# Four Strassen pairs per down projection, norms on ScalarE, beta by accumulating transfers, wider up-stage operations, and a planner that replays its order

## The chip, the cores and the metric

The kernel runs on one core of one Trainium2 chip. The metric is the device time of one execution in microseconds (us), given as the median of several runs. A core has five engines that work side by side: PE (matrix products, with PEld for its weight loads), DVE (VectorE), ACT (ScalarE), POOL (GpSimd) and SP (SyncE, which here only issues transfers). Each works through its own queue in order and waits on semaphores for the others.

## The reference

Two decoder layers over 256 tokens of width 1024, all in float32. `alpha` is a constant; every sub-layer ends in a layer norm with a gain (gamma) and a bias (beta).

```python
for i in range(2):
    y = chunked_gmlp(x, ...) if i == 0 else moba_attention(x, ...)
    x = layer_norm(DN_ALPHA * x + y, ln_mix_g[i], ln_mix_b[i])
    y = conv_ffn(x, f_w_up[i], f_conv_w[i], f_conv_b[i], f_w_down[i])
    x = layer_norm(DN_ALPHA * x + y, ln_ffn_g[i], ln_ffn_b[i])

def conv_ffn(x, w_up, conv_w, conv_b, w_down):   # w_up 1024 x 5632, w_down 2816 x 1024
    h = x @ w_up
    hc = conv_b + sum of three causally shifted h, each times its conv_w[j]
    g, val = jnp.split(hc, 2, axis=-1)
    return (jax.nn.gelu(g) * val) @ w_down
```

## The kernel before, in words

**Products of float32.** Every float32 operand of a large product is split into a high part and a low remainder of a faster type (`split`: ACT copies to the high part, DVE subtracts to get the low one). A product is then three matmuls: high x high, high x low, low x high. The weights arrive in chunks of 1 MB (`prep`), each 128 x 2048, are split into `whi` and `wlo`, and are held five chunks ahead. The activations are split too and live in `xt` (inputs of the up stages) or `rr` (inputs of the down stages).

**Stages.** PE runs a_v, a_u, a_out (mixer A), f_up0, f_dn0 (ConvFFN of layer 0), b_v, b_qk, b_o (mixer B), f_up1, f_dn1. A down projection (`project_out`) sums over 22 tiles `k` of 128 rows for two token halves `t` and two column halves. Two neighbouring `k` are a pair, so there are 11 pairs, and an ordinary pair takes 2 x 2 x 2 x 3 = 24 matmuls of 512 columns.

**Strassen pairs.** Pairs listed in `FAST` take seven products in place of eight (`unit`, 21 matmuls). For these, DVE builds four sums of weight blocks (`weight_forms`, four forms of 512 columns) and four sums of token blocks (`token_forms`), and both are split like any operand. The forms of the weights take the place of `xt` or of the used-up start of `rr` (`used_up`). Products that belong to no single output are kept in four PSUM banks (`sums`) and are added to the residual rows `x` by `combine` after the last fast pair.

**Up stages.** `conv_up` makes four output tiles of 256 columns per group (`cols_times`, ten groups a stage). Each lands in a PSUM bank as two halves that `join` adds (ACT copies one half, DVE adds the other). `gate` then applies the convolution (one ACT operation and two DVE operations per tile), the gelu, the product and the split.

**Inner norms.** After a_out, f_dn0 and b_o, `stats` computes mean and variance on DVE, POOL takes the power -0.5 (line L571), and `ln_back` normalizes the rows on DVE (`ts`, line L325), lets PE transpose them (L306), and lets ACT apply gamma and beta from `lncol` in the transposed layout and split the result to `xt`. `rest` later multiplies the rows by gamma and adds beta on DVE, since the rows are the next residual.

**What sets the order.** Nothing is issued when it is written. `Plan` records every operation with its engine, a cost in ns and what it depends on. `emit` gives PE's bulk matmuls in their written order a due time, walks the dependencies back to give all others theirs, then simulates the five queues once and emits the operations in the order of their simulated starts. PE work marked `fill` (transposes, attention scores) is fitted in when ready. Line L300 is where all matmuls are issued, L306 all transposes, L312 all ACT operations, L318 and L322 DVE's two-input ones, L329 SP's loads.

Of the kernel before, what the change touches and what calls it, by code (L numbers as in the profile page):

```python
# [53 lines left out]
FAST = {"f_dn0": (4, 7), "f_dn1": (4, 5, 7)}  # L54
# [24 lines left out]
class Op:  # L79
    __slots__ = ("i", "eng", "ns", "emit", "deps", "bufs", "fill", "due", "start", "end", "table", "nbytes", "rank")  # L80


class Plan:
# [4 lines left out]
    LATE = {"pe": 200.0, "act": 140.0, "dve": 130.0, "pool": 200.0, "sp": 910.0}  # L88
# [39 lines left out]
    def emit(self):  # L128
        ops = self.ops
        for o in ops:  # L130
            for b in o.bufs:
                for q in b.prev:
                    o.deps.update(x for x in q.ops if x is not o)
            assert all(d.i < o.i for d in o.deps), "a group waits for one recorded after it"

        t = 0.0
        for o in ops:
            o.due = math.inf
            if o.eng == "pe":
# [11 lines left out]
        succ, left = {}, {}
        for o in ops:
            left[o] = len(o.deps)
            for d in o.deps:
                succ.setdefault(d, []).append(o)
        engines = ("pe", "act", "dve", "pool", "sp")
        free = dict.fromkeys(engines, 0.0)
        cand = {e: [] for e in engines}
        bus, table = 0.0, None
        order = []  # L160
        bulk = [o for o in ops if o.eng == "pe" and not o.fill]
        nb = 0

        def ready(o):
            return max([0.0] + [d.end + self.lag(d, o) for d in o.deps])

        for o in ops:
            if not left[o]:
                cand[o.eng].append((0.0, o))
        while len(order) < len(ops):  # L170
            best = None
            for e in engines:
                c = cand[e]
                if e == "pe":
                    c = [x for x in c if x[1].fill or (nb < len(bulk) and x[1] is bulk[nb])]
                if not c:
                    continue
                s0 = min(max(free[e], r) for r, _ in c)
                now = [x for x in c if max(free[e], x[0]) <= s0 + 1.0]
                if e == "pe":  # L180
                    pick = min(now, key=lambda x: (not x[1].fill, x[1].due))
                else:
                    pick = min(now, key=lambda x: x[1].due + (x[1].ns if e in ("act", "dve") else 0.0))
                    for x in c:
                        s = max(free[e], x[0])
                        if x[1].due < pick[1].due and s0 < s < s0 + pick[1].ns and \
                                s + x[1].ns <= pick[1].due and x[1].due < s0 + pick[1].ns:
                            pick = x
                s = max(free[e], pick[0])
                if best is None or s < best[0]:  # L190
                    best = (s, e, pick)
            s, e, pick = best
            o = pick[1]
            cand[e].remove(pick)
            if o.eng == "pe" and not o.fill:
                nb += 1
            o.start = s
            if e == "sp":
                bus = max(bus, s + 1100.0) + o.nbytes / 415.0
                free[e] = max(s + 475.0, bus - 1500.0)  # L200
                o.end = bus
            else:
                extra = 0.0
                if o.table and o.table != table:
                    extra, table = 1300.0, o.table
                o.end = free[e] = s + o.ns + extra
            order.append(o)
            for x in succ.get(o, ()):
                left[x] -= 1
                if not left[x]:  # L210
                    cand[x.eng].append((ready(x), x))
        order.sort(key=lambda o: (o.start, o.i))
        for o in order:
            o.emit()
# [15 lines left out]
def trunk_kernel(ctx: ExitStack, tc: tile.TileContext, a: dict, out: bass.AP):  # L230
# [43 lines left out]
    banks = [ps.tile([P, HALF], F32, name=f"bank{i}") for i in range(BANKS)]  # L274
# [3 lines left out]
    def bank(long=False):  # L278
# [378 lines left out]
    def project_out(name, nk, at, xold, li, rows_i, wait=REST, first=None):  # L657
# [55 lines left out]
        def combine():  # L713
# [14 lines left out]
            for b in sums:  # L728
                done_with(b, 0)
# [414 lines left out]
```

## Time and profile before

| what | value |
|---|---|
| runs, us | 559.74, 557.76, 557.22 (median 557.76) |
| profiled execution: span from first to last instruction | 555.0 us |
| lowest and median run over that span | 2.2 us and 2.8 us |
| PE busy | 547.0 us, 99% |
| DVE busy | 498.9 us, 90% |
| ACT busy | 378.3 us, 68% |
| DMA, mean | 200 GB/s |

The time of the profiled execution itself is known only as its span; what lies around it is taken as the difference to the median, 2.8 us. Busy time counts an instruction from its start to its written result, and neighbours on one engine overlap a little, so a mean duration is longer than the step from one start to the next.

### The profile page before, as it was taken

To read this page: it belongs to the slowest core of one execution; us is meant where nothing else is said; L and a number is where in the kernel's file an instruction comes from. 1 tells how busy PE (TensorE), PEld (TensorE's weight loads), DVE (VectorE), ACT (ScalarE), POOL (GpSimd) and SP (SyncE) were. 2 spreads that over 40 slices of the span, in tenths; PEclk is the share of its full clock that TensorE was granted. 3 is DMA by queue.
4 is the path that set the end of the run, shared out by engine and by line. 5 is a ranking of instruction groups with operands and counts; after the bars stand their busy time and mean duration, and the time that the engine had idled before them with its cause. 6 is when DMAs were issued, how large, how long until landed. Compare 5 with 4: busy or idle time off the path is not lost.

```text
span 555.0 us, 8220 instructions
## 1 busy us (share of the span) xinstructions
PE 547.0 (99%) x2968; PEld 468.8 (84%) x2968; DVE 498.9 (90%) x967; ACT 378.3 (68%) x718; POOL 11.3 (2%) x17
## 2 busy tenths in 40 slices
PE   9999999999999999999999999999999999999994
PEld 6888888898988988888888888888898988988884
DVE  6889889999999999989948898889898999999997
ACT  6846586877877884645668877587767877776510
POOL 0010000000000000001000000000000000000001
PEclk9999999999999999999999999999999999999998
DMA  8996626686545524764565363416765466444602
GB/s 317 413 335 238 230 92 228 227 308 224 208 172 188 191 77 153 285 227 152 191 263 191 110 251 138 174 70 233 298 232 223 155 227 227 153 151 153 220 9 76
DMA packets 20105, 111.12 MB, mean 200 GB/s; under 512 B 2256, under 2 KB 5600, under 8 KB 7904
## 3 DMA queue, kind: packets, MB, share of 16 engines
q1 hardware_dynamic: 19488, 109.94, 54.7%
q10 hardware_dynamic: 576, 0.66, 0.3%
q8 instruction: 23, 0.38, 0.3%
q14 instruction: 18, 0.15, 0.1%
HBM read 109.52 MB, written 1.07 MB: 199 GB/s over the span
## 4 chain that ended last, share of the span: by engine, by line
PE 99%; DVE 1%; issue 0%; DVEq 0%
PE bank L300 96%; PE bank L306 2%; DVE x L322 0%; DVE stat L563 0%; DVEq L1140 0%; DVE stat L569 0%
## 5 line engine op out<-in xcount | busy, mean ns | idle before, releaser
L318 DVE TENSOR_TENSOR wlo<-raw,whi 128x1024 fp32r<-128x1024 f32 (+2 forms) x205 | 216.6, 1079 | 19.9 <-ACT whi L312 13.3
L312 ACT ACTIVATE whi<-raw 128x1024 fp32r<-128x1024 f32 (+2 forms) x205 | 185.1, 941 | 61.5 <-DMA raw<-in_f_up 22.2
L300 PE MATMUL bank<-xt,whi 128*128 128x512 f32 x832 | 195.9, 391 | 0.0
L300 PEld LDWEIGHTS bank<-xt,whi 128*128 128x128 f32 x832 | 154.2, 188 | 30.6
L300 PE MATMUL bank<-whi,rr 128*128 128x512 f32 (+1 forms) x428 | 134.1, 387 | 0.0
L300 PEld LDWEIGHTS bank<-xt,wlo 128*128 128x128 f32 x832 | 103.1, 192 | 2.1
L300 PE MATMUL bank<-xt,wlo 128*128 128x256 f32 x832 | 104.8, 284 | 0.0
L300 PEld LDWEIGHTS bank<-whi,rr 128*128 128x128 f32 x428 | 80.0, 188 | 16.2 <-issue 0.2
L300 PE MATMUL bank<-wlo,rr 128*128 128x512 f32 (+1 forms) x214 | 82.6, 386 | 0.0
L322 DVE SCALAR_TENSOR_TENSOR ff<-ff,convc 128x255 f32<-128x255 f32 (+1 forms) x160 | 70.4, 476 | 0.3 <-ACT ff L312 0.2
L312 ACT ACTIVATE ff<-bank 128x256 f32<-128x256 f32 (+2 forms) x126 | 49.3, 400 | 27.1 <-PE bank L300 19.9
L300 PE MATMUL bank<-whi,xt 128*128 128x512 f32 (+1 forms) x196 | 60.7, 390 | 0.0
L318 DVE TENSOR_TENSOR ff<-bank,ff 128x256 f32<-128x256 f32 (+1 forms) x110 | 45.5, 431 | 8.5 <-ACT ff L312 7.7
L312 ACT ACTIVATE ff<-ff,convc 128x256 f32<-128x256 f32 x80 | 45.0, 592 | 3.0 <-DVE ff L318 2.9
L300 PEld LDWEIGHTS bank<-wlo,rr 128*128 128x128 f32 x214 | 40.2, 188 | 7.9
L300 PEld LDWEIGHTS bank<-whi,xt 128*128 128x128 f32 x196 | 36.4, 188 | 8.3 <-ACT whi L312 1.2
L300 PE MATMUL bank<-wlo,xt 128*128 128x512 f32 (+1 forms) x98 | 36.4, 387 | 0.0
L312 ACT ACTIVATE ff<-bank,lncol 128x128 f32<-128x128 f32 x48 | 18.7, 459 | 17.5 <-PE bank L306 17.5
L318 DVE TENSOR_TENSOR ff<-ff 128x256 f32<-128x256 f32 (+3 forms) x74 | 30.3, 431 | 0.3 <-ACT ff L312 0.2
L312 ACT ACTIVATE ff<-ff 128x256 f32<-128x256 f32 x52 | 20.4, 411 | 11.3 <-DVE rr L318 6.8
L318 DVE TENSOR_TENSOR xt<-ff,xt 128x256 fp32r<-128x256 f32 (+3 forms) x32 | 21.8, 691 | 4.1 <-ACT xt L312 4.0
L312 ACT ACTIVATE rr<-ff 128x256 fp32r<-128x256 f32 (+3 forms) x50 | 21.3, 442 | 5.2 <-DVE ff L318 5.1
(75 smaller groups left out, 360.7 us busy)
## 6 DMA issues: line engine op xcount, KB each, us to landing
raw<-in_f_up SPq DMA_DIRECT2D x44, 1024.0 KB, 4.8
raw<-in_f_dn SPq DMA_DIRECT2D x20, 1024.0 KB, 4.8
raw<-in_b_qk SPq DMA_DIRECT2D x8, 1024.0 KB, 4.9
lnrow<-in_lnrow SPq DMA_DIRECT2D x5, 1024.0 KB, 6.6
raw<-in_a_u SPq DMA_DIRECT2D x4, 1024.0 KB, 8.4
raw<-in_a_out SPq DMA_DIRECT2D x4, 1024.0 KB, 6.0
raw<-in_b_v SPq DMA_DIRECT2D x4, 1024.0 KB, 4.7
raw<-in_b_o SPq DMA_DIRECT2D x4, 1024.0 KB, 4.9
```

What stands on the lines that cost most here:

```text
L300: nc.tensor.matmul(o, l, x, start=start, stop=stop, skip_group_check=mixed)
L306: nc.tensor.transpose(o, x, ident.ap)
L312: plan.op("act", ns, lambda: nc.scalar.activation(o, x, func, **kw), r, w, table=table)
L318: dve(70 + 1.04 * flat(x), lambda: nc.vector.tensor_tensor(o, x, y, op=op), r, w)
L322: lambda: nc.vector.scalar_tensor_tensor(o, x, s, y, op0=op0, op1=op1), r, w)
```

## The change

It does six things.

1. `FAST` names four pairs in each down projection, (3, 5, 6, 7), where it was two in f_dn0 and three in f_dn1. The raw weights of these pairs go to homes of their own (`home`): two places in `ff` and the tile `lnrow`, loaded in two transfers of 512 KB. `weight_forms` now works in place on the raw weights, in fewer and wider operations, and is recorded at points set by `FORMS`. `ln_rows` of a down projection is therefore loaded after `combine`.
2. The inner norms are made by ACT: DVE computes `shift` = -mean x rstd (one column), and ACT computes rstd x x + shift.
3. After a_out and b_o, beta is added to the rows by POOL, as a transfer from DRAM that accumulates into the rows; the multiplication by gamma stays on DVE.
4. In the up stages a group's four tiles lie in four neighbouring banks (`four_banks`); one ACT copy and one DVE addition of 1024 columns join them, and gelu, product and split work on 512 columns.
5. `build_bias` is recorded before f_up0 in place of after it.
6. `Plan.emit` orders 4 x 40 times, each time replays the order under four cases of speed, moves operations that PE waited for to earlier due times, and keeps the order with the smallest mean time. Matmuls, transposes and transfers have measured costs (`took`) beside the old ones.

```diff
-FAST = {"f_dn0": (4, 7), "f_dn1": (4, 5, 7)}
+FAST = {"f_dn0": (3, 5, 6, 7), "f_dn1": (3, 5, 6, 7)}
+HOMES = (0, 1, 2, 0, 1)
+FORMS = ((0, None), (1, 3), (0, 3), (1, 5))
 ...
+    def weight_forms(name, j):
+        key = name, FAST[name][j]
+        (r0, r1), f, (b11, b12, b21, b22) = raw_sums[key]
+        h, l = used_up(0, KT) if FORMS[j][0] else xt_new()
+        tt(f[:, b22:b12 - 1:b12 - b22, :], f[:, b12:b12 + 1, :].to_broadcast([P, 2, HALF]),
+           f[:, b22:b11 - 1 if b11 else None:b11 - b22, :], ALU.add, ...)
+        tt(f[:, b11, :], f[:, b22, :], f[:, b11, :], ALU.add, ...)
+        tt(f[:, b21, :], f[:, b11, :], f[:, b21, :], ALU.add, ...)
+        for n, raw in ((1, r1), (0, r0)):
+            split(...)
 ...
     def ln_back(r, st, mean, rstd, rows, t, li, h, l, waits, wait):
+        shift = st.ap[:, 28:29]
+        dve(70, lambda: nc.vector.scalar_tensor_tensor(shift, mean, -1.0, rstd, op0=ALU.mult, op1=ALU.mult), ...)
         for k0 in range(0, KT, step):
-            ts(x[:, sl], x[:, sl], mean, rstd, ALU.subtract, ALU.mult, ...)
+            act(x[:, sl], x[:, sl], AF.Identity, ..., bias=shift, scale=rstd)
         def rest():
             rb, rv = rows
+            if li != 1:
+                for o in (0, HALF):
+                    tt(x[:, sl], x[:, sl], rv[:, 0, sl], ALU.mult, ...)
+                beta = bass.AP(tensor=src.tensor, offset=..., ap=[[0, P], [1, D]])
+                plan.op("pool", 1000.0, lambda: nc.gpsimd.dma_start(x, beta, accum_op=ALU.add), ...)
+                return
 ...
+        if units:
+            weight_forms(name, 0)
+        def more(c):
+            for j, (_, after) in enumerate(FORMS[:len(units)]):
+                if c == after:
+                    weight_forms(name, j)
 ...
         for i in range(2, FT, 2):
-            tiles4 = [(bank(), *sub(name, i + j // 2, j % 2)) for j in range(4)]
-            cols_times(tiles4, h, l)
+            whole, four = four_banks()
+            cols_times([(b, *sub(name, i + j // 2, j % 2)) for j, b in enumerate(four)], h, l)
+            act(c3, b3[:, :, S:], AF.Copy, four, [c], psum=True)
+            tt(c3, b3[:, :, :S], c3, ALU.add, [*four, c], [c])
 ...
+        for seed in range(TRIALS):
+            for _ in range(ROUNDS):
+                order = self.order(self.dues(urge), seed)
+                runs = [self.replay(order, *case) for case in CASES]
+                mean = sum(r[0] for r in runs) / len(runs)
+                if best is None or mean < best[0]:
+                    best = mean, order
 ...
+                for _, waits in runs:
+                    for k, ns in waits:
+                        urge[k] += rnd.uniform(0.3, 1.0) * ns + rnd.uniform(0.0, 300.0)
```

Three places of the order follow. First PE in f_dn0 at pair 3. Before, the pair is ordinary, and these are the twelve matmuls of its first tile `k` (`whi_69`, `wlo_79`); twelve of the same kind on `whi_70` and `wlo_80` follow.

```order
L300 MATMUL bank_105<-whi_69,rr 128x512
L300 MATMUL bank_105<-wlo_79,rr 128x512
L300 MATMUL bank_105<-whi_69,rr 128x512
L300 MATMUL bank_106<-whi_69,rr 128x512
L300 MATMUL bank_106<-wlo_79,rr 128x512
L300 MATMUL bank_106<-whi_69,rr 128x512
L300 MATMUL bank_107<-whi_69,rr 128x512
L300 MATMUL bank_107<-wlo_79,rr 128x512
L300 MATMUL bank_107<-whi_69,rr 128x512
L300 MATMUL bank_108<-whi_69,rr 128x512
L300 MATMUL bank_108<-wlo_79,rr 128x512
L300 MATMUL bank_108<-whi_69,rr 128x512
```

The same pair after, whole: `small` holds the token forms, `xt_87` the weight forms.

```order
L358 MATMUL bank<-whi_70,rr 128x512
L358 MATMUL bank<-wlo_80,rr 128x512
L358 MATMUL bank<-whi_70,rr 128x512
L358 MATMUL bank<-whi_70,small 128x512
L358 MATMUL bank<-wlo_80,small 128x512
L358 MATMUL bank<-whi_70,small 128x512
L358 MATMUL bank<-whi_69,rr 128x512
L358 MATMUL bank<-wlo_79,rr 128x512
L358 MATMUL bank<-whi_69,rr 128x512
L358 MATMUL bank<-xt_87,rr 128x512 x3
L358 MATMUL bank<-xt_87,small 128x512 x9
```

Twenty-four matmuls have become 21, and the last twelve of them need the weight forms. Second the norm of the second token half after a_out. Before, on DVE (`stat_94` is that half's statistics, `x_89` its rows):

```order
L569 BN_AGGR stat_94<-stat_94 128x2
L318 TENSOR_TENSOR wlo_83<-raw_85,whi_73 128x512
L325 TENSOR_SCALAR x_89<-x_89,stat_94 128x256 x4
L318 TENSOR_TENSOR wlo_83<-raw_85,whi_73 128x512
L318 TENSOR_TENSOR wlo_84<-raw_85,whi_74 128x512
L318 TENSOR_TENSOR xt_87<-ff,xt_87 128x2x128 x2
```

After, on ACT (`ff<-bank,lncol` is gamma and beta on the transposed rows):

```order
L370 ACTIVATE x_89<-x_89,stat_94 128x256 x4
L370 ACTIVATE ff<-bank,lncol 128x128 x2
L370 ACTIVATE xt_87<-ff 128x2x128
L370 ACTIVATE ff<-bank,lncol 128x128 x2
L370 ACTIVATE xt_87<-ff 128x2x128
L1007 COPY ff<-bank 128x512
L370 ACTIVATE ff<-bank,lncol 128x128 x2
L370 ACTIVATE xt_87<-ff 128x2x128
```

The four pieces of the norm have moved from DVE to ACT, where they stand ahead of the operations on the transposed rows. Third POOL's queue from the first norm of a_out on. Before:

```order
L571 TENSOR_TENSOR stat_91<-stat_91,nhalf 128x1
L571 TENSOR_TENSOR stat_92<-stat_92,nhalf 128x1
L571 TENSOR_TENSOR stat_93<-stat_93,nhalf 128x1
L571 TENSOR_TENSOR stat_94<-stat_94,nhalf 128x1
L571 TENSOR_TENSOR stat_91<-stat_91,nhalf 128x1
```

After:

```order
L655 TENSOR_TENSOR stat_91<-stat_91,nhalf 128x1
L655 TENSOR_TENSOR stat_92<-stat_92,nhalf 128x1
L655 TENSOR_TENSOR stat_93<-stat_93,nhalf 128x1
L696 DMA x_88<-in_lnrow 128x1024
L655 TENSOR_TENSOR stat_94<-stat_94,nhalf 128x1
L696 DMA x_89<-in_lnrow 128x1024
```

The accumulating transfer of the first token half now stands ahead of the second half's power.

More of the change, by code (lines that the diff above doesn't have):

```diff
@@ L1 @@
 import math
+import random
 from contextlib import ExitStack
@@ L151, in emit @@
[L151 to L158, printed above, removed]
-        bus, table = 0.0, None
[L160 to L201, printed above, removed]
@@ new lines, in emit, with dues @@
+        for k in best[1]:
+            ops[k].emit()
+    def dues(self, urge):
+        ops, t = self.ops, 0.0
+        due = [math.inf] * len(ops)
+        for k, o in enumerate(ops):
+            if o.eng == "pe":
+                due[k] = t
+                t += o.took
+        for k in range(len(ops) - 1, -1, -1):
+            due[k] = min(due[k], t) - urge[k]
+            for d, late in self.deps[k]:
+                p = ops[d]
+                due[d] = min(due[d], due[k] - late - p.took - p.tail - (2000.0 if p.eng == "sp" else 0.0))
+        return [due[k] if o.rank is None else o.rank - 1e6 for k, o in enumerate(ops)]
@@ new lines, in replay @@
+    def replay(self, order, rate, first, act, dve):
+        ops, waits = self.ops, []
+        end = [0.0] * len(ops)
+        free = {"pe": BEGIN, "act": 0.0, "dve": 0.0, "pool": 0.0, "sp": 0.0}
+        by = {"act": act, "dve": dve}
+        bus, table = 0.0, None
+        for k in order:
+            o = ops[k]
+            e = o.eng
+            f = s = free[e]
+            for d, late in self.deps[k]:
+                s = max(s, end[d] + late)
+            if e == "pe" and s > f + 50.0 and s > 20000.0:
+                waits.append((k, s - f))
+            if o.nbytes:
+                bus = max(bus, s + first + (900.0 if e == "pool" else 0.0)) + \
+                    o.nbytes / 1000.0 / (rate if o.nbytes >= 1 << 20 or s < 80000.0 or e != "sp" else 0.72 * rate)
+                end[k], free[e] = bus, s + (380.0 if e == "sp" else o.took)
@@ L202, in emit @@
             else:
-                extra = 0.0
                 if o.table and o.table != table:
[L205 to L214, printed above, removed]
+                    s, table = s + 1300.0, o.table
@@ L284, in bank, with four_banks @@
         return b
+    def four_banks():
+        free = [i for i in (0, 4) if not any(x[2] for x in bank_of[i:i + 4])]
+        i = min(free, key=lambda i: max(x[0] for x in bank_of[i:i + 4]))
+        return psum[:, i * HALF:(i + 4) * HALF], [bank(at=j) for j in range(i, i + 4)]
     def done_with(b, age=None):
@@ L369, in trunk_kernel, with home @@
     xrows = [Buf(t) for t in xs_]
+    raw_sums = {}
+    def home(i):
+        name, c = stream[i]
+        j = HOMES[FAST[name].index(c)]
+        if j < 2:
+            pair, t, at = [place("ff", o + SUB * j, SUB) for o in (0, 5 * HALF)], ff, (0, 1, 5, 6)
+            at = [x + 2 * j for x in at]
+        else:
+            old, t, at = rowring.held[0], rowring.tiles[0], (0, 1, 2, 3)
+            group = rowring.held[0] = Buf(old.ap, [old])
+            pair = [Buf(old.ap[:, n * SUB:(n + 1) * SUB], [old]) for n in range(2)]
+            for b in pair:
+                b.ops = group.ops
+        raw_sums[name, c] = pair, t.rearrange("p (a n) -> p a n", n=HALF), at
+        return [(b, b.ap, 0) for b in pair]
     def raw_of(i):
-        if is_fast(i) and stream[i][1] == FAST[stream[i][0]][-1]:
-            early = place("ff", 2560, CH)
-        elif i == 2:
+        if is_fast(i):
+            return home(i)
+        if i == 2:
             early = place("ff", 2560, CH)
@@ L442, in token_forms @@
         split((h, [0], h.ap), (l, [0], l.ap), (s, range(4), s.ap))
-        return h, l
+        tokens[key] = h, l
     def prep(i):
         name, c = stream[i]
-        if i > 1 and is_fast(i - 2):
-            weight_forms(i - 2)
         raw = raw_of(i)
-        if name != "a_v":
+        if is_fast(i):
+            for n, (b, _, _) in enumerate(raw):
+                load(b.ap, a[name][c][:, n * SUB:(n + 1) * SUB], [(b, range(4))])
+        elif name != "a_v":
             load(raw[0][0].ap, a[name][c], [(raw[0][0], range(8))])
```

257 lines of the change are left out of this document (171 added, 86 removed).

## The prediction

> **What bounds the kernel now.** I read the page first: its busy line and the chain of work that ended last.
>
> ```profile
> PE 547.0 (99%) x2968; PEld 468.8 (84%) x2968; DVE 498.9 (90%) x967; ACT 378.3 (68%) x718; POOL 11.3 (2%) x17
> ...
> PE 99%; DVE 1%; issue 0%; DVEq 0%
> ```
>
> The chain is PE from one end to the other. A busy PE could still hide waits, since its busy time includes pipelined ends, so I asked for PE's waits, for the chain in order of time, and for busy time by stage (columns: stretch, its length, busy time and count of PE, PEld, DVE, ACT, POOL, granted clock, DMA share, GB/s).
>
> ```profile
> PE bank L300 <- PEq L1137: 0.8, 1, 0.8
> ```
> ```profile
> 379.89 167.98 PE bank L300 x902
> ...
> 547.89 0.43 DVE x L322
> ```
> ```profile
> 87.30:198.80 111.50, 111.50 (x646) 98.86 (x645) 105.75 (x195) 87.05 (x161) 0.00 (x0) 1.00 0.58 209
> 198.80:258.40 59.60, 59.60 (x269) 49.41 (x268) 55.80 (x90) 34.02 (x53) 1.35 (x1) 1.00 0.51 190
> ...
> 378.20:489.70 111.50, 111.50 (x646) 98.84 (x645) 104.92 (x194) 88.48 (x164) 0.00 (x0) 1.00 0.61 217
> 489.70:547.90 58.20, 58.15 (x268) 48.37 (x266) 57.09 (x97) 25.61 (x37) 1.05 (x1) 1.00 0.32 118
> 547.90:555.00 7.10, 0.00 (x0) 0.00 (x0) 4.07 (x9) 0.00 (x0) 1.05 (x1) 0.66 0.22 74
> ```
>
> PE's only wait is 0.8 us at the start. From there it runs without a gap to 547.9, and a tail of 7.1 us follows. The rows are f_up0, f_dn0, f_up1, f_dn1 and the tail; the clock is full in every stage. So time falls only with PE instructions, with the head, or with the tail; and every new wait of PE is added in full. DVE is the engine that could cause one: 95%, 94%, 94% and 98% busy in the four stages.
>
> **The change part by part.**
>
> *Matmuls.* Three more pairs become fast (two in f_dn0, one in f_dn1), each with 21 matmuls for 24: nine fewer, all of 512 columns. The price is the step from one to the next:
>
> ```profile
> 514.16 2.20 PE L300 MATMUL bank<-xt,small 128*128 128x512 f32 x9
> 516.20 0.39 PE L300 MATMUL bank<-whi,rr 128*128 128x512 f32 x1
> ```
>
> Nine take 2.20, one 0.39, so a step is (2.20 - 0.39) / 8 = 0.226 us, and nine are 2.04 us. Nothing lies beside them: **-2.04**.
>
> [...] The trace shows PE busy 99% and its weight loads busy 84%. [...] By the wait rows it is -2.04, and I take these, since a PE with room would show waits.
>
> *Transposes.* The new order cuts five groups of transposes in two. A first matmul behind transposes takes 0.48 where others take 0.39, so five more cost at most 0.45. But eight transposes hold PE from 79.09 to 79.88, 0.79 us, or 0.10 each, and a shorter group may drop as much at its end. Between 0 and 0.45, I take 0.
>
> ```profile
> 79.09 1.03 PE L306 MATMUL bank<-ident,x 128*128 128x128 f32 x8
> ...
> 79.88 0.48 PE L300 MATMUL bank<-whi,xt 128*128 128x512 f32 x1
> ```
>
> *DVE's ledger.* Groups by shape (busy, mean ns), and two in a row:
>
> ```profile
> L318 DVE TENSOR_TENSOR wlo<-raw,whi 128x1024 fp32r<-128x1024 f32 x153 | 183.3, 1217 | 16.6 <-ACT whi L312 10.1 <-PE bank L300 4.5 <-ACT ff L312 1.2
> L318 DVE TENSOR_TENSOR ff<-bank,ff 128x256 f32<-128x256 f32 x104 | 41.6, 417 | 8.4 <-ACT ff L312 7.7
> L318 DVE TENSOR_TENSOR x<-x,lnrow 128x512 f32<-128x512 f32 x24 | 15.6, 683 | 0.0
> L318 DVE TENSOR_TENSOR ff<-ff 128x128 f32<-128x128 f32 x20 | 5.2, 282 | 0.0
> L325 DVE TENSOR_SCALAR x<-x,stat 128x256 f32<-128x256 f32 x12 | 4.1, 407 | 0.9 <-POOL stat L571 0.9
> L325 DVE TENSOR_SCALAR x<-x,stat 128x512 f32<-128x512 f32 x6 | 3.0, 545 | 1.3 <-POOL stat L571 1.3
> ```
> ```profile
> 526.88 2.35 DVE L318 TENSOR_TENSOR xt<-ff,xt 128x1024 fp32r<-128x1024 f32 x2
> ```
>
> Two of 1.22 in a row take 2.35, so one occupies 0.09 less than it lasts: 1.13 for 1024 columns, 0.60 for 512, 0.33 for 256, 0.20 for 128; the norms 0.32 and 0.46. Gone are the norms, 12 x 0.32 + 6 x 0.46 = 6.6, and beta, 8 x 0.60 = 4.8. In 20 groups of the up stages four joins become one of 1024 columns. No row has it on a bank; its bounds are 1.13 and four of 256 columns, 1.32, and 1.13 is the nearer in shape: 20 x (1.32 - 1.13) = 3.8. Product and split become 512 wide: 20 x 2 x 0.06 = 2.4. Together -17.6. Each new fast pair adds its blocks 1.13 + 2 x 0.60, their splits 2 x 1.13, tokens 0.33 + 2 x 0.20 + 0.60, and saves 0.53 of a chunk's split: 5.4, three times 16.2. With six one-column shifts and the wider splits of the kept tiles, about 1, DVE's sum stays where it was. None of it is time as long as PE does not wait.
>
> By stage it moves. f_up0 with f_dn0 had 105.75 + 55.80 = 161.6 of 171.1 us. They gain 10.8 and lose 3.1 in the up stage and 2.4 of beta: 166.9 of 169.7, 98%. f_up1 with f_dn1 stays at 162 of 169.0, 96%. f_dn1 ran at 98% without a wait, so this is covered, with nothing to spare in f_dn0. Take the cover away and the forms are late.
>
> *Norms on ACT.* This lengthens a chain that PE waits for. After a_out and b_o the first half's up-stage matmuls, 24 x 0.226 = 5.4 us, hide the second half's norm.
>
> ```profile
> 77.11 0.89 POOL L571 TENSOR_TENSOR stat<-stat,nhalf 128x1 f32<-128x1 f32 x1 [8.35 <-DVE stat L569]
> 78.03 1.38 DVE L325 TENSOR_SCALAR x<-x,stat 128x256 f32<-128x256 f32 x4 [0.44 <-POOL stat L571]
> ...
> 79.51 1.15 ACT L312 ACTIVATE ff<-bank,lncol 128x128 f32<-128x128 f32 x3 [0.15 <-PE bank L306]
> ...
> 80.55 0.42 ACT L312 ACTIVATE xt<-ff 128x256 fp32r<-128x256 f32 x1
> 80.86 0.46 ACT L312 ACTIVATE ff<-bank,lncol 128x128 f32<-128x128 f32 x1
> 81.00 0.43 DVE L318 TENSOR_TENSOR xt<-ff,xt 128x256 fp32r<-128x256 f32 x1 [0.39 <-ACT xt L312]
> 81.11 0.62 PE L300 MATMUL bank<-whi,xt 128*128 128x512 f32 x2
> ```
> ```profile
> L312 ACT ACTIVATE ff<-ff,convc 128x256 f32<-128x256 f32 x80 | 45.0, 592 | 3.0 <-DVE ff L318 2.9
> L566 DVE TENSOR_SCALAR stat<-stat 128x1 f32<-128x1 f32 x10 | 1.5, 147 | 0.1
> ```
>
> The second half's first matmul is the later of the two at 81.11, at 81.34; its high part was ready at 80.97: 0.37 us to spare. After, a shift of 0.15 (nearest row, L566) and the ACT piece of 0.59 (same shape and operands as the convolution's) end at 78.00 + 0.03 + 0.15 + 0.03 + 0.59 = 78.80, where DVE's piece ended at 78.44. All four ACT pieces stand ahead of the `lncol` operations: about 0.5 each, so `lncol` begins near 80.2. Two of these (0.80 together) and the split (0.42, less overlap) bring the high part to 81.3. That is just in time. But the first transposes now stand two matmuls earlier, at 79.09 - 0.45 = 78.64, against 78.80 and a handover: some 0.2 us of wait, at two places, **+0.4**. Ends: 0, if the work ahead comes earlier, and 0.8 a place, all of ACT's extra (4 x (0.50 - 0.32) + 0.15). After f_dn0 six tiles `k`, 8.2 us, cover the chain.
>
> *Beta by POOL.* Transfer and power share POOL's queue. The transfer waits for DVE's two multiplications by gamma; behind it waits the second half's power, behind that DVE's shift, ACT's norm and PE. Sixteen matmuls, 3.6 us, lie between its place in the order and the power's. No row has such a transfer on POOL; POOL's operations lie between 0.1 and 1.1 us, and SP's issues take less:
>
> ```profile
> L525 POOL TENSOR_SCALAR_AFFINE_SELECT ff<-ff 128x1024 f32<-128x1024 f32 x1 | 1.1, 1091 | 25.6 <-DMA ff<-in_wsT 25.6
> ```
> ```profile
> raw<-in_f_dn SPq DMA_DIRECT2D x20, 1024.0 KB, 4.8
> ...
> lnrow<-in_lnrow SPq DMA_DIRECT2D x5, 1024.0 KB, 6.6
> ```
>
> I take 1.1, the row of the same 1024 columns, hidden in the 3.6. Landing, some 7 us by the `lnrow` row, is hidden by the up stage of over 100 us ahead of the rows' next use.
>
> *Homes and SP.* Eight more issues on SP. A home is free when the up stage or the forms before have left it; ordinary loads queue behind. A load takes 4.8 us and chunks are held five ahead, 5 x 5.4 = 27 us: nothing. Head and tail do the same operations: 0.
>
> **Sum.** -2.04 + 0.4 = -1.64. The span goes from 555.0 to 553.4, and with the 2.8 us to the median of the runs, 557.76 becomes **556.1**.
>
> **Rivals.**
>
> *The forms come too late* (slower). The forms of pairs 5 and 7 go to storage that pairs 3 and 5 free, so they cannot all be made ahead. In f_dn1 the margin was already used up:
>
> ```profile
> 528.44 0.84 PE L300 MATMUL bank<-xt,rr 128*128 128x512 f32 x3
> 529.12 2.26 PE L300 MATMUL bank<-xt,small 128*128 128x512 f32 x9
> ```
>
> DVE's last split of the forms (the pair from 526.88) ends at 529.23, and the second of these nine needs it at 529.35: they take 2.26 in place of 2.20. If f_dn1's added 5.4 is not made ahead, DVE needs 57.1 + 5.4 = 62.5 in 57.5 us, 5.0 late; with -2.04 that is 560.7. It undoes the gain from 2.04 us of waits, and is slower by 0.5% from 4.8. Against it: the sums over both stages above leave room.
>
> *POOL's transfer holds up the power.* If it takes longer than 3.6 us on POOL, the rest is added twice: at 5 us 2 x 1.4 - 1.64, or 558.9. Against it stand POOL's rows, all near 1 us. [...] No run here shows such a transfer.
>
> *PE is bound by its supply after all*, and waits where matmuls were: 557.8. [...] Against it the single wait row.
>
> *Better than the sum*: no wait at the norms, and a head whose 0.6 us of stretched matmuls close up too: 557.76 - 2.04 - 0.6 = 555.1 or a little below. Those rows show six steps near 0.1 too long:
>
> ```profile
> 4.65 0.49 PE L300 MATMUL bank<-wlo,xt 128*128 128x256 f32 x2
> 4.98 0.72 PE L300 MATMUL bank<-whi,xt 128*128 128x256 f32 x4
> ```
>
> **How the numbers follow.** My forecast (PE full but for 0 to 1 us of waits, 555.1 to 556.8) has 0.62, late forms 0.20 (half of it beyond 4.8 us), POOL's transfer 0.06, supply 0.05, better 0.07. What a measurement can tell from no change is 0.5%, 2.8 us: below 555.0 is faster, above 560.5 slower. Only "better" reaches the first, half of "late forms" the second: 0.07, 0.83, 0.10. The range leaves out "better" and the later half of the late forms: 554.9 to 558.6.
>
> **What would show it.** Nine fewer matmuls of 512 columns at steps of 0.226; PE's waits under 1 us in all, at the first transposes of the second half after a_out and b_o; DVE near 499 us; four transfers on POOL near 1 us each. Wrong would be waits of PE on `xt`, `rr` or `small` at pairs 5 to 7, or on `x` behind POOL.

## The result, and the profile after

The median is 562.99 us (561.73 to 564.39, four runs) against 557.5 us of the kernel before, run beside it: a ratio of 1.0095 (1.0066 to 1.0124). A second series gave 562.49 us and 1.0100 (1.0085 to 1.0115). The change made the kernel 5.5 us slower; forecast were 556.1, no change, and a range from 554.9 to 558.6. The profiled execution has a span of 562.5 us.

The busy line and the chain's shares by engine, of the changed kernel's page:

```profile
PE 550.2 (98%) x2959; PEld 466.8 (83%) x2959; DVE 502.2 (89%) x871; ACT 386.3 (69%) x645; POOL 15.5 (3%) x21
...
PE 56%; DVE 17%; ACT 6%; DMA 4%; issue 2%; POOL 0%; DVEq 0%; ACTq 0%; POOLq 0%; SPq 0%
```

PE has nine instructions less, as said (2959 for 2968), and is busy longer. Before, the chain was PE from end to end; now a quarter of it runs over DVE, ACT and transfers. What PE and its weight loads waited for (us in total, times, longest):

```profile
PE bank L364 <- ACT x L370: 2.0, 4, 1.1
PE bank L358 <- ACT small L370: 1.3, 2, 1.0
PE bank L358 <- PEq L1255: 0.8, 1, 0.8
PE bank L358 <- DVE small L376: 0.3, 1, 0.3
PE bank L358 <- DVE wlo L376: 0.2, 1, 0.2
```
```profile
PEld bank L364 <- ACT x L370: 4.7, 7, 1.5
...
PEld bank L364 <- ACT ff L1007: 0.7, 2, 0.5
```

The first line of each is the inner norms: transposes (L364) that wait for the normalized `x`. In the down projections `small` holds token forms: 1.0 us of the second line and the whole fourth line are forms that came late in f_dn1. The other 0.3 us of the second line is a wait in b_qk, where `small` holds an operand of mixer B.

These rows are not the whole loss. A better measure is the length of each stage, from its first matmul on PE's timeline to the first of the next. For the first columns of f_up0 the two ends are, in the changed kernel and in the kernel before:

```profile
76.50 0.39 PE L358 MATMUL bank<-whi,xt 128*128 128x512 f32 x1
...
89.50 0.84 PE L358 MATMUL bank<-xt,whi 128*128 128x512 f32 x3
```
```profile
75.01 0.39 PE L300 MATMUL bank<-whi,xt 128*128 128x512 f32 x1
...
87.26 0.84 PE L300 MATMUL bank<-xt,whi 128*128 128x512 f32 x3
```

That is 13.00 us for 12.25: 0.75 lost, by the same matmuls. Taken so for all stages, the changed kernel's PE ends 7.4 us later:

| place | us more than before |
|---|---|
| norms: a_out 0.77, first columns of f_up0 0.75, b_v 0.53, b_o -0.02, first columns of f_up1 0.43 | 2.46 |
| down projections, with the norm behind f_dn0: f_dn0 1.01, f_dn1 1.17, though nine matmuls (2.04) are gone | 2.18 |
| b_qk | 1.74 |
| a_v with what is ahead of it 0.78, other columns of f_up1 0.29, a_u -0.06, f_up0 -0.02 | 0.99 |

With the saved matmuls added back, the two down projections lost 4.2 us. In f_dn0 this holds a wait for the norm behind it: from the start of the last matmul, 254.76, to the first transpose, 256.27, pass 1.51 us where a step is 0.23, so the wait is 1.28. (Single waits are counted so from here on.) The norms thus lost 3.7 us in all, and the down projections themselves 2.9: 1.09 in f_dn0 and 1.85 in f_dn1.

The second execution of the same kernel (e20 below) has 2.47, 2.07, 0.08 and 0.81: the first two rows belong to the kernel, b_qk's was not there again. Busy time by stage (columns as in the prediction): the first columns, the other columns of f_up0, f_dn0, and the same of layer 1.

```profile
76.50:89.50 13.00, 12.61 (x62) 10.09 (x60) 10.66 (x21) 12.42 (x28) 1.77 (x2) 1.00 0.74 194
89.50:201.00 111.50, 111.50 (x645) 98.77 (x644) 106.01 (x165) 82.22 (x116) 0.00 (x0) 1.00 0.59 217
201.00:261.60 60.60, 59.25 (x262) 47.72 (x260) 57.90 (x76) 36.93 (x50) 1.35 (x1) 1.00 0.48 165
...
371.40:384.10 12.70, 12.54 (x62) 10.08 (x61) 10.71 (x21) 12.56 (x29) 1.70 (x2) 1.00 0.65 184
384.10:495.90 111.80, 111.70 (x646) 98.73 (x645) 107.00 (x166) 83.94 (x118) 0.00 (x0) 1.00 0.60 219
495.90:555.20 59.30, 57.96 (x265) 47.70 (x263) 56.22 (x76) 27.01 (x33) 1.05 (x1) 1.00 0.32 108
```

Three places show how it is lost. First, the norm behind f_dn0, first token half, on the timeline (a bracket is idle time and what ended it):

```profile
252.72 0.69 DVE L647 BATCH_NORM_STATS2 stat<-x 128x6 f32<-128x512 f32 x1
...
253.82 1.35 POOL L655 TENSOR_TENSOR stat<-stat,nhalf 128x1 f32<-128x1 f32 x1 [167.17 <-DVE stat L653]
255.21 0.16 DVE L681 SCALAR_TENSOR_TENSOR stat<-stat 128x1 f32<-128x1 f32 x1 [0.46 <-POOL stat L655]
...
255.40 1.52 ACT L370 ACTIVATE x<-x,stat 128x512 f32<-128x512 f32 x2 [0.45 <-DVE stat L681]
256.27 0.42 PEld L364 LDWEIGHTS bank<-ident,x 128*128 128x128 f32 x4 [1.54 <-ACT x L370]
```

The power takes 1.35 us here. The new planner costs it at 465 ns, and puts the transposes where they would then fit. The planner before had the same 465 ns for powers of 0.70 to 1.35 us, and PE did not wait, so the figure alone does no harm. Second, f_dn1 at pair 7, and the pieces of the chain in order of time around it (start, us, what):

```profile
532.37 0.39 PE L358 MATMUL bank<-whi,rr 128*128 128x512 f32 x1
533.76 0.50 PE L358 MATMUL bank<-whi,small 128*128 128x512 f32 x1 [1.00 <-ACT small L370]
534.09 0.40 PE L358 MATMUL bank<-wlo,small 128*128 128x512 f32 x1
534.83 0.50 PE L358 MATMUL bank<-whi,small 128*128 128x512 f32 x1 [0.34 <-DVE small L376]
```
```profile
385.89 75.88 PE bank L358 x436
461.80 0.97 DVE wlo L376
...
532.96 1.22 DVE rr L376
534.18 0.61 DVE small L376
534.83 20.40 PE bank L358 x100
```

From 461.8, still in f_up1, to 534.8 the chain runs mostly over DVE: what is late at pair 7 reaches back some 70 us. Third, b_qk, where one transfer took 7.30 us (4.8 in the median), with the high part behind it, and then PE:

```profile
291.13 7.30 DMA raw<-in_b_qk
298.51 1.06 ACT whi L370
300.39 6.74 PE bank L358 x40
```

### The profile page after: what moved, and what is told of

It reads as the page before. It is cut to its first block, busy times and chain, and to the rows that moved or that the text cites. A ratio compares the mean times of both kernels' runs of the same rounds, so it can differ in the third digit from the quotient of the medians.

```text
span 562.5 us, 8052 instructions
## 1 busy us (share of the span) xinstructions
PE 550.2 (98%) x2959; PEld 466.8 (83%) x2959; DVE 502.2 (89%) x871; ACT 386.3 (69%) x645; POOL 15.5 (3%) x21
## 4 chain that ended last, share of the span: by engine, by line
PE 56%; DVE 17%; ACT 6%; DMA 4%; issue 2%; POOL 0%; DVEq 0%; ACTq 0%; POOLq 0%; SPq 0%
PE bank L358 54%; DVE wlo L376 6%; DVE ff L376 4%; DMA raw<-in_b_qk 3%; DVE ff L380 2%; ACT whi L370 2%; PE bank L364 2%; ACT ff L370 1%; ACT x L370 1%; DVE rr L376 1%; DVE x L380 1%; DMA raw<-in_f_dn 1%; DVE small L376 1%; DVE xt L376 1%; DMA ff<-in_f_dn 1%
## 5 line engine op out<-in xcount | busy, mean ns | idle before, releaser
L376 DVE TENSOR_TENSOR wlo<-raw,whi 128x1024 fp32r<-128x1024 f32 (+2 forms) x193 | 201.9, 1080 | 19.1 <-ACT whi L370 18.7
L370 ACT ACTIVATE whi<-raw 128x1024 fp32r<-128x1024 f32 (+2 forms) x193 | 173.4, 938 | 36.1 <-DMA raw<-in_f_up 9.0
L380 DVE SCALAR_TENSOR_TENSOR ff<-ff,convc 128x254 f32<-128x254 f32 (+1 forms) x160 | 66.4, 477 | 1.6 <-ACT ff L370 1.3
L370 ACT ACTIVATE ff<-bank 128x256 f32<-128x256 f32 (+3 forms) x66 | 39.4, 614 | 19.4 <-PE bank L358 14.8
L376 DVE TENSOR_TENSOR ff<-ff 128x512 f32<-128x512 f32 (+3 forms) x70 | 41.1, 596 | 3.1 <-ACT ff L370 1.3
L376 DVE TENSOR_TENSOR ff<-bank,ff 128x256 f32<-128x256 f32 (+2 forms) x50 | 37.9, 771 | 2.9 <-ACT ff L370 2.8
L370 ACT ACTIVATE rr<-ff 128x512 fp32r<-128x512 f32 (+2 forms) x36 | 24.7, 697 | 21.0 <-DVE ff L376 21.0
L370 ACT ACTIVATE ff<-ff 128x512 f32<-128x512 f32 (+1 forms) x32 | 17.3, 547 | 21.2 <-DVE ff L380 19.5
L376 DVE TENSOR_TENSOR rr<-ff,rr 128x512 fp32r<-128x512 f32 (+2 forms) x36 | 27.5, 774 | 1.1 <-ACT rr L370 0.7
L655 POOL TENSOR_TENSOR stat<-stat,nhalf 128x1 f32<-128x1 f32 x10 | 9.7, 975 | 492.8 <-DVE stat L653 492.8
```

Of the source, the lines that this page charges most:

```text
L370: plan.op("act", ns, lambda: nc.scalar.activation(o, x, func, **kw), r, w, table=table)
L376: dve(70 + 1.04 * flat(x), lambda: nc.vector.tensor_tensor(o, x, y, op=op), r, w)
L380: lambda: nc.vector.scalar_tensor_tensor(o, x, s, y, op0=op0, op1=op1), r, w)
L655: plan.op("pool", 465, lambda: nc.gpsimd.tensor_tensor(rstd, mv[:, 1:2], nhalf.ap, op=ALU.pow), [(st, ["mv"]), nhalf], [(st, ["rstd"])])
```

## The experiments

Theories. A: the new planner, which costs PE at its real step, leaves no reserve for the other engines. A2: only the power's cost and the cases of speed, under which an order is replayed, are too kind. B: four pairs ask for more of DVE than there is. C: norms on ACT make the chain longer. Each kernel's planner makes an order of its own, so its time also holds the luck of that order. "Norms" and "down" are sums of stage lengths as in the table above, in us more than before, one profile each; in "down" the saved matmuls (2.04 us with four pairs, 0.68 with three and three) are not added back, and a wait for the norm behind f_dn0 is counted in it. The changed kernel's cases are "kind": transfers at 0.395 KB per ns or more, ACT and DVE at most 1% slower. The "unkind" ones of e13 go down to 0.37 KB per ns, and to 2% slower. (Where an expectation calls these figures shares of a full rate, read KB per ns: the planner divides a transfer's KB by them.)

| kernel | pairs | norms on | power, ns | cases | ratio (95%) | norms | down |
|---|---|---|---|---|---|---|---|
| changed | 4, 4 | ACT | 465 | kind | 1.0095 (1.0066-1.0124) | 2.46 | 2.18 |
| e20, the same | 4, 4 | ACT | 465 | kind | 1.0100 (1.0085-1.0115) | 2.47 | 2.07 |
| e8, other draw | 4, 4 | ACT | 465 | kind | 1.0127 (1.0107-1.0148) | 3.40 | 1.57 |
| e3 | 4, 4 | ACT | 1360 | kind | 1.0106 (1.0087-1.0124) | 2.63 | 3.90 |
| e5 | 4, 4 | DVE | 465 | kind | 1.0131 (1.0112-1.0149) | 1.97 | 5.99 |
| e19 | 4, 4 | DVE | 1360 | kind | 1.0208 (1.0187-1.0228) | 0.50 | 10.11 |
| e9 | 4, 4 | ACT | 1360 | unkind | 1.0127 (1.0111-1.0143) | 2.39 | 4.05 |
| e12 | 4, 4 | DVE | 1360 | unkind | 1.0142 (1.0127-1.0157) | 0.53 | 6.81 |
| e14 | 3, 3 | DVE | 1360 | unkind | 1.0059 (1.0041-1.0077) | 0.25 | 2.94 |
| e4 | 2, 3 | ACT | 465 | kind | 1.0100 (1.0084-1.0116) | 2.55 | 3.38 |
| e15 | 2, 3 | DVE | 465 | kind | 1.0144 (1.0131-1.0157) | 1.53 | 5.99 |
| e16 | 2, 3 | DVE | 1360 | kind | 1.0059 (1.0044-1.0074) | 0.24 | 2.52 |
| e17 | 2, 3 | DVE | 465 | unkind | 1.0048 (1.0036-1.0060) | 1.77 | -0.26 |
| e11 | 2, 3 | ACT | 1360 | unkind | 1.0076 (1.0050-1.0102) | 1.73 | 0.06 |
| e13 | 2, 3 | DVE | 1360 | unkind | 1.0010 (0.9999-1.0021) | 0.21 | 0.10 |
| e18, other draw | 2, 3 | DVE | 1360 | unkind | 1.0031 (1.0016-1.0046) | 0.25 | 1.37 |

**e1_old_planner.**
```diff
-                order = self.order(self.dues(urge), seed)
-                runs = [self.replay(order, *case) for case in CASES]
+        while len(order) < len(ops):
+            best = None
+            for e in engines:
```


> All of the changed kernel's operations, ordered by the planner of the kernel before (one simulated order, PE planned at 215.8 us per 1000 matmuls of 512 columns where the trace shows 226, SP's handover 910 ns). The changed kernel has 9.5 us of PE waits that the kernel before did not have: 0.8 in the head, 3.7 at the inner norms, 1.7 in b_qk, 2.7 late forms in the two down projections, 0.3 at the first group of f_up1, the rest in split transposes. Theory A (the new planner leaves no reserve): most of these go, PE's new waits come to 3 us or less, and the time is 555.5 to 558. Theory B (DVE has too much work ahead of and in the down projections): the waits on forms and sums in f_dn0 and f_dn1 stay (2.7 us and the 1.3 at the norm behind f_dn0), 560 to 563. Theory C (norms on ACT make the chain too long): 0.5 us or more at each of the first transposes after a_out, f_dn0 and b_o stay, 558 to 561.

571.17 us, ratio 1.0229 (1.0210 to 1.0249). No theory expected that. f_dn0 and f_dn1 are 6.4 and 7.4 us longer than before; in each PE waits once for `rr`, 3.3 and 4.0 us, and with each wait the granted clock falls to 0.50, for 6.7 and 3.3 us. The norms' stages lose 3.9 us. The new planner is not what loses; the new operations lose more without it.

**e2_new_planner.** The kernel before, with the class `Plan` and the costs `took` of the changed one.

> All operations of the kernel before, ordered by the changed kernel's planner. Theory A: PE's waits appear here too, 3 us or more of them at the inner norms and in b_qk, and the time is 560 to 563 against 557.5. Theories B and C: PE waits as little as before (under 1.5 us) and the time is 556.5 to 558.5, since neither the two and three fast pairs nor DVE's norms ask for more than before.

572.74 us, 1.0277 (1.0253 to 1.0301): slower, as A had it, but far beyond its 560 to 563 and by other places. f_dn0 and f_dn1 are 6.7 us longer each, with a wait of 3.6 us near the start of f_dn0 and of 4.2 inside f_dn1, and a granted clock of 0.50 for over 3 us with each; the norms' stages lose 1.3 us in all, b_qk nothing. In this order the kernel also computes something else than the reference (relative error 0.21; where it goes wrong stays open), so little rests on its time: at most that the new planner does not suit the operations before as it stands.

**e7_pe_reserve.**
```diff
-            took = sum(max(107.0, flat(x) / 2.4 + 13.4) if ...
+            took = sum(max(107.0, flat(x) / 2.4) + 2.5 if ...
-        return 0.0 if d.eng == o.eng else self.LATE[d.eng] + (60.0 if o.eng == "pe" else 0.0)
+        return 0.0 if d.eng == o.eng else self.LATE[d.eng]
```


> The changed kernel whose planner costs PE as the kernel before did: a matmul of 512 columns at 215.8 ns in place of 226.7, and no 60 ns more for a handover to PE. This gives every other engine a reserve of about 5% of PE's time (25 us over the span) in the plan. Theory A: 3 to 6 us of PE's waits go, 557 to 560. Theory B: the plan cannot make DVE's work smaller, the waits stay where they are within 1 us: 562 to 564. Theory C: the waits at the norms stay, 561 to 563.

572.53 us, 1.0265 (1.0248 to 1.0282), where A expected 557 to 560; the loss is again in f_dn0 (4.3) and f_dn1 (6.9), and the norms' stages lose 5.1. With e1 this ends theory A as far as PE's step goes: a plan with too quick a PE is worse here.

**e4_fewer_pairs.**
```diff
-FAST = {"f_dn0": (3, 5, 6, 7), "f_dn1": (3, 5, 6, 7)}
+FAST = {"f_dn0": (3, 5), "f_dn1": (3, 5, 6)}
```


> The changed kernel with as many fast pairs as before, (3, 5) in f_dn0 and (3, 5, 6) in f_dn1: nine more matmuls of 512 columns (2.04 us) and some 16 us less of DVE work. Theory B: the waits of f_dn0 and f_dn1 and the 1.3 us at the norm behind f_dn0 go (4 us) against 2.04 more of matmuls, so 560.5 to 561.5. Theories A and C: the waits at the norms and in b_qk stay (5 us), those in the down projections get smaller: 561.5 to 564. If the four pairs were right and only their order wrong, this run is no faster than the changed kernel.

563.38 us: no faster than the changed kernel. f_dn1 lost most of its waits, but f_dn0 got new ones, 1.0 and 1.3 us for `rr`. Fewer pairs alone do not mend it: B alone falls.

**e3_pow_cost.**
```diff
-        plan.op("pool", 465, lambda: nc.gpsimd.tensor_tensor(rstd, ..., op=ALU.pow),
+        plan.op("pool", 1360, lambda: nc.gpsimd.tensor_tensor(rstd, ..., op=ALU.pow),
```


> The changed kernel with one number of its planner altered: POOL's power is planned at 1360 ns in place of 465 (the trace shows it at 0.55 to 1.36 us, 1.36 at both places behind f_dn0). Theory A2 (the planner puts the transposes too early because it takes the power for half as long as it is): the waits at the first transposes (0.53, 0.55, 1.28, 0.16, 0.32 us) shrink to 1 us in all, the time is 560 to 561.5. Theory C (ACT's norm makes the chain longer than the matmuls that can stand ahead of it, whatever the plan): the waits move from the transposes to the matmuls behind them, and the time stays at 562 to 564.

563.28 us, as C expected. The wait behind f_dn0 shrank from 1.28 to 0.74 and a_out loses 0.17 for 0.77, but the first columns of the up stages lose 1.04 and 0.91 in place of 0.75 and 0.43: the loss moved behind the transposes. f_dn0 and f_dn1 lose 1.7 us more than in the changed kernel.

**e5_norms_dve.**
```diff
-            act(x[:, sl], x[:, sl], AF.Identity, ..., bias=shift, scale=rstd)
+            ts(x[:, sl], x[:, sl], mean, rstd, ALU.subtract, ALU.mult, ...)
```


> The changed kernel with the inner norms back on DVE: no shift, four or two operations of DVE where ACT had them. The planner orders anew. Theory C: the waits at the first transposes drop by 0.2 us or more at each of six places, 1.5 to 2.5 us in all, and the time is 560.5 to 561.5. Theory A2: the power is still planned at half its length, so they drop by the shift's 0.15 only, and the time is 562 to 563.5. Theory B (DVE has no room): 6.6 us more on DVE make the late forms later, 564 or more.

564.79 us, as B expected: the norms' stages gained 0.5 us, the down projections lost 3.8 more.

**e8_other_draw.**
```diff
-            rnd = random.Random(seed)
+            rnd = random.Random(seed + 100)
```


> The changed kernel, its planner's random numbers drawn from other seeds: the same operations and costs, another of the orders that its replay holds for equally good. It says how much of any difference between kernels with orders of their own is luck. If the losses are the plan's rule (A2, B, C), the same places wait and the time is 562 to 564; if they are the luck of this order, it lies outside 561 to 565, by 3 us or more at other places.

564.44 us, above the 562 to 564 expected of a rule, with waits at the same norms (0.53, 0.54, 2.00, 0.17, 0.40, 0.61 us). An order's luck is of the size of 1 to 2 us; that the norms lose is not luck.

**e13_mixed.** The edits of e3, e4 and e5, and other cases (KB per ns of a transfer, its delay in ns, factors on ACT's and DVE's costs):
```diff
-CASES = ((0.403, 2200.0, 1.0, 1.0), (0.395, 2400.0, 1.0, 1.0), (0.4, 2300.0, 1.0, 1.005), (0.4, 2500.0, 1.01, 1.0))
+CASES = ((0.403, 2200.0, 1.0, 1.0), (0.37, 2600.0, 1.0, 1.0), (0.39, 2400.0, 1.0, 1.02), (0.38, 2500.0, 1.02, 1.01))
```


> The changed kernel with norms on DVE, as many fast pairs as before ((3, 5) and (3, 5, 6)), the power planned at 1360 ns, and four cases of speed that are less kind (transfers at 0.37 to 0.403 of full rate in place of 0.395 to 0.403, DVE and ACT up to 2% slower). Wide up stages, beta on POOL and the new planner stay. If pairs, norms and costs make up the loss (A2, B and C together), 5 us of waits go for 2.04 more of matmuls: 558 to 560. If what remains of the change costs by itself (beta on POOL, wide operations, the planner), 561 or more.

557.98 us: the loss is gone. So beta on POOL, the wide up stages and the new planner together cost nothing here that can be measured, and the loss came from pairs, norms and costs. The kernel has as many fast pairs as before, so it has no matmuls to gain by either. PE's only wait row, and f_up0 with f_dn0, f_up1 with f_dn1:

```profile
PE bank L358 <- PEq L1252: 0.8, 1, 0.8
```
```profile
88.10:199.60 111.50, 111.50 (x645) 98.78 (x644) 105.50 (x162) 82.71 (x118) 0.89 (x1) 1.00 0.63 222
199.60:259.40 59.80, 59.70 (x268) 49.19 (x267) 51.89 (x66) 32.17 (x43) 0.56 (x1) 1.00 0.54 189
379.20:490.70 111.50, 111.50 (x646) 98.75 (x645) 106.49 (x166) 84.99 (x120) 0.84 (x1) 1.00 0.63 223
490.70:548.80 58.10, 58.09 (x268) 48.41 (x266) 51.23 (x68) 25.41 (x31) 1.05 (x1) 1.00 0.32 115
```

DVE has 51.9 and 51.2 us of work in the down projections where the changed kernel has 57.9 and 56.2.

**e9_costs_alone.** e13 with four pairs and norms on ACT.

> One corner of a square around e13_mixed, which stood 0.1% above the kernel before, with a wait of 0.26 us at one norm. Here four fast pairs and norms on ACT stay, as in the changed kernel; the power at 1360 ns and the less kind cases of speed are those of e13_mixed. If the planner's costs were what was wrong (theory A2), 557 to 559, below e13_mixed by up to 2 us of matmuls. Theory B (four pairs ask for more of DVE than there is): PE still waits 2 us or more for forms in the two down projections, 561 to 564. Theory C adds waits of 1 us or more at the norms.

563.74 us, as B expected. f_dn1's waits, and busy time by stretch with the granted clock (the third number from the right):

```profile
531.26 0.50 PE L358 MATMUL bank<-rr 128*128 128x512 f32 x1 [0.95 <-ACT rr L370]
533.30 1.03 PE L358 MATMUL bank<-rr 128*128 128x512 f32 x2 [1.54 <-DVE rr L376]
534.13 3.55 PE L358 MATMUL bank<-rr,small 128*128 128x512 f32 x9
```
```profile
528.00:530.00 2.00, 2.00 (x11) 1.58 (x9) 1.97 (x4) 0.79 (x1) 0.00 (x0) 1.00 0.49 127
...
534.20:535.80 1.60, 1.60 (x5) 1.25 (x4) 1.60 (x3) 1.09 (x2) 0.00 (x0) 0.50 0.00 0
```

After two waits close together the clock is 0.50, and nine matmuls take 3.55 us in place of 2.20: the waits cost more than they last.

**e11_acts_norms.** e13 with norms on ACT.

> Second corner: e13_mixed with the norms on ACT as in the changed kernel, and as many fast pairs as before. Theory C: against e13_mixed 1.5 us or more, all of it at the first transposes of a_out, f_dn0 and b_o, or at the matmuls right behind them: 559.5 to 561. If ACT's norms are free once the pairs are fewer and the costs honest: 557.5 to 558.5.

560.5 us, as C expected, with the loss behind the transposes: the first columns of f_up0 and f_up1 are 0.60 and 0.87 us longer, by their bounds as above; f_up0's other columns lose 0.43. ACT's part of the norm costs PE 1.5 us against e13 even where pairs and costs are mended.

**e12_four_pairs.** e13 with four pairs.

> Third corner: e13_mixed with four fast pairs in each down projection. Nine matmuls less are 2.04 us. Theory B: they bring waits for forms of more than that in f_dn0 and f_dn1, 559 to 563. If four pairs pay once the plan is honest: 555.5 to 557.

565.1 us, B's direction and beyond its range: f_dn0 and f_dn1 lose 1.39 and 5.42 where e13 loses nothing. Same planner, same costs, same norms: the four pairs bring 6.7 us, and the 2.04 saved are in it. Not all of this is waiting: two waits of 1.50 and 0.95 us stand close together in f_dn1, and from 536.1 to 539.4 us the granted clock is 0.50, worth some 1.7 us as in e9.

**e15_kind_cases.** e13 with the power at 465 ns and the kind cases.

> e13_mixed planned as the changed kernel is: the power at 465 ns and the four kind cases of speed; norms on DVE, as many pairs as before. Theory A2: the norms wait again, 1.5 us or more, with 1 to 2 us for forms or chunks elsewhere: 560 to 562. If fewer pairs and DVE's norms were enough: 557.5 to 559.

565.08 us, as A2 had it but beyond its range. Both the norms (1.53) and the down projections (5.99) wait.

**e14_three_pairs.** e13 with `"f_dn0": (3, 5, 6)`.

> e13_mixed with one fast pair more in f_dn0, three in each down projection. Three matmuls less are 0.68 us, DVE gets 5.4 us more ahead of pair 6 of f_dn0; f_dn1 is as in e13_mixed. Theory B by degree: f_dn0 waits 1 to 3 us for forms or for the norm behind it, f_dn1 does not wait, 558.5 to 560.5. If only the fourth pair is too much: 557 to 558. If the pairs matter by luck of the order: no wait in f_dn0 or as much in f_dn1.

560.57 us (560.29 without one execution of 3137 us). f_dn0 loses 1.27 + 0.68 = 1.95 us, as B has it by degree; f_dn1, which was left as it was, lost 1.67, which B does not explain. An order's luck can: e18 below loses 1.25 in f_dn1 by another draw alone. The loss does grow with the pairs, two, three, four in f_dn0: 0.1, 2.9, 6.8 us over both down projections.

**e16_power_alone.** e13 with the kind cases.

> e13_mixed with the kind cases of speed; only the power is planned at 1360 ns. If the power's length was the planner's error, 557.5 to 559. If the reserve that the unkind cases give to transfers, DVE and ACT was what counted, PE waits for chunks and forms as in e15_kind_cases (565.1): 562 to 565, without waits at the norms.

560.2 us, between the two expectations: no waits at the norms, 2.52 in the down projections.

**e17_cases_alone.** e13 with the power at 465 ns.

> e13_mixed with the power planned at 465 ns as in the changed kernel; the unkind cases stay. If the reserve of the cases counts, PE waits only at the norms, 0.3 to 0.6 us at each of four places, 558.5 to 560. If the power's length counts, 562 or more.

560.04 us, as the cases' reading had it: nothing in the down projections, 1.77 around the norms. So at the norms only the power's cost counted (0.24 in e16, 1.77 here). In the down projections both did: e15 lost 5.99 there, e16 2.52, this one nothing. Why the power's cost counts there is not shown. The unkind cases are a reserve for ACT, DVE and transfers, so in this wider sense theory A's want of reserve was real.

**e18_mixed_draw.** e13 with other seeds.

> e13_mixed with the planner's random numbers from other seeds. If e13_mixed is what its costs make of it, 557 to 559.5 and PE's waits below 1 us in all behind the head. If it was a lucky order, 561 to 565 like the other corners.

558.82 us: not a lucky order alone, though 1.37 us came back in the down projections.

**e19_norms_mended.** The changed kernel with the edits of e3 and e5.

> The changed kernel (four pairs, kind cases of speed) with norms on DVE and the power planned at 1360 ns. By PE's stages, either of the two alone left 2 us of loss around the norms. If both together mend them, the first columns of f_up0 and f_up1 are as long as before (12.25 us each, within 0.1), a_out, b_v and b_o lose 0.5 us or less in all, and the down projections keep their loss of 2 to 6 us: 560 to 564. If the norms' loss has to do with the pairs, the first columns stay 0.3 us or more too long.

The norms went as expected (0.50; the first columns are 0.05 and 0.03 longer), the rest did not: the down projections lose 10.1 us, and the time is 568.12. With four pairs, DVE's norms made the down projections worse each time (e5 against the changed kernel by 3.8 us, e19 against e3 by 6.2, e12 against e9 by 2.8). Part of e19's loss is the clock's: it is 0.50 from 242.3 to 245.6 and from 535.9 to 542.5 us, and some 19 matmuls there step at 0.43 us for 0.23, about 4 us.

**e20_again.** The changed kernel itself.

> The changed kernel itself, a second time. If the 1.7 us in b_qk belong to its order, b_qk is again 1.5 us or more longer than before (57.6 against 56.1), and the time is 561.5 to 564.5. If a late transfer of one execution made them, b_qk is within 0.5 us of before, and the two groups of run times (spans of 560.0 and 562.5) are these two kinds of execution.

562.49 us; b_qk is 0.08 longer than before, not 1.74. In its chain PE alone fills that stretch:

```profile
269.95 36.21 PE bank L358 x199
```

So the 7.30 us transfer was one execution's, and the two groups of spans, 560.0 and 562.5, can be these two kinds; two profiles don't prove it.

**What the square shows.** The norms' stages lose 0.2 to 0.5 us in the six kernels that have both DVE's norms and the longer power, and 1.5 to 3.4 in the ten that lack either. The down projections lose next to nothing (-0.3 to 0.1, once 1.4) in the four that have both few pairs and unkind cases, and 1.6 to 10.1 in the twelve others. Each kernel is one order in one profile, and another draw moved a sum by 0.6 to 1.3 us (e8, e18), so the pattern counts and not a small difference between two corners.

## Why the prediction was wrong, point by point

- **Matmuls, -2.04: right.** 2959 for 2968, and the step is still 0.226. All that followed had to be less than this.
- **Transposes, 0: right.** Eight in one group held PE for 0.79 us; two groups of four that wait for nothing take 0.35 each, and each first matmul behind them 0.09 more.
- **Norms on ACT, +0.4: the size failed, it was 3.7.** The failed step is that I looked for the wait only at the second half's transposes after a_out and b_o. The first half after a_out waited 0.53 as well, and the norm behind f_dn0, which I called covered by 8.2 us of tiles, waited 1.28: its cover is only worth what the planner leaves of it, and it planned the power at 465 ns. The rest lies behind the transposes, in the first columns, where ACT's pieces stand ahead of its other work (e11 against e13: 1.5 us). I quoted the power's row of 0.89 us and did not set it against the 465 ns in the code. ACT alone is not the cause: with the norms on DVE and the power still at 465 ns (e5) these stages lost 1.97 us.
- **DVE's ledger, "covered": failed; 2.9 in place of 0.** The sums were near (499 said, 502.2 measured; 166.9 and 162 said for the two layers, 163.9 and 163.2 measured; the wide join steps at 1.13), but the conclusion was not. That f_dn1 ran at 98% without a wait showed that one order met its dues, not that there was room. DVE had 8.2 us idle over f_up0 and f_dn0, and PE lost 1.1 us in f_dn0 all the same, apart from the norm behind it, and 1.85 in f_dn1. A ledger over two stages says whether work fits, not when a form is ready.
- **Beta by POOL, hidden: right.** The four issues take 0.87 to 1.02 us (1.1 said), and the next power waited for DVE's statistics, not for the transfer, as here in the second half of a_out:

```profile
75.31 1.02 POOL L696 DMA_DIRECT2D x<-in_lnrow  x1 [5.63 <-DVE x L376]
78.68 0.89 POOL L655 TENSOR_TENSOR stat<-stat,nhalf 128x1 f32<-128x1 f32 x1 [2.35 <-DVE stat L653]
```

- **Homes, SP, head and tail, 0:** no loss of a fixed size. The load of 7.30 us cost b_qk 1.74 us in one execution, in spite of the chunks held ahead, and nothing in the other. a_v was 0.78 and 0.51 us longer in the two executions of the changed kernel. In the first, four matmuls of 256 columns took 1.22 us (at 5.46), in the second 0.73 (at 5.05), as at the end of this document in e14.
- **The rivals.** "Forms come too late" (560.7) is the nearest: it named the place and the engine. It took the loss as 5.0 us in f_dn1 alone; it was 1.1 in f_dn0 and 1.85 in f_dn1, and the norms lost 3.7 on top, so that its time is near by other terms. "POOL's transfer" and "better" did not come. "Supply" did not either: PE has nine matmuls less at the same step, and what it lost are waits for other engines and for one transfer.

No kernel here is faster than the one before. The most to gain is 2.04 us, 0.4%. By the prediction's estimate of 5.4 us a pair, the three pairs put some 16 us on DVE; no run had four pairs and that much less on DVE, so whether they can pay stays open.

## What to carry to other kernels

Where one engine is full without a wait, ask of each added operation not whether its engine has time in the stage but at which instant its result is due, and what stands ahead of it in that queue. A planner that finds no waits by its own costs is only as good as its kindest cost: compare each cost with the row of the profile that has it, the small operations on the way to a wait first. Several small optimizations that each lean on the same engine have to be tried together as well as one by one: here none of the three single edits (e3, e4, e5) made the changed kernel faster, and those three with the unkind cases took off 5 us.

## What the hardware showed that was not expected

PE's waits had a second price in some runs. In e9, after two waits of 0.95 and 1.54 us within 3.1 us, the granted clock was 0.50, and matmuls stepped at 0.43 us for some 3.5 us, 1.7 us more. In the changed kernel it stayed at 1.00 after 1.28 us behind f_dn0 and after 1.16 in f_dn1, and in e4 after 1.26 and 0.95 within 2.7 us. Why e4's two waits left it at 1.00 and e9's did not stays open.

In the head the same step of 0.43 us (four from 8.03 to 9.73 below) shows without the clock's row telling it. In e14 a head transfer landed late:

```profile
6.58 1.22 PE L358 MATMUL bank<-whi,xt 128*128 128x256 f32 x4 [1.08 <-ACT whi L370]
...
8.03 1.91 PE L358 MATMUL bank<-whi,xt 128*128 128x512 f32 x4
9.73 0.88 PE L358 MATMUL bank<-wlo,xt 128*128 128x512 f32 x2
```
```profile
8.00:10.00 2.00, 2.00 (x7) 1.61 (x6) 1.91 (x4) 1.35 (x3) 0.00 (x0) 1.00 1.02 408
```

Four matmuls take 1.91 us where four take 1.09 in the kernel before, at a granted clock given as 1.00; a_v grew by 3.1 us in that execution. And POOL's power of one column took from 0.55 to 1.36 us by place, for the same shape; what sets it was not tried.
